# In-place operand sums with a second x staging set, and a half-precision rotary step of the queries, in a two-layer hybrid diffusion kernel

## Chip, cores, metric

The kernel runs on the 8 cores of one Trainium2 chip (dies: cores 0 to 3 and 4 to 7). The metric is device microseconds of the slowest core. Executions of this program fall into two states: fast, and slow, where one die or both run at a lower granted TensorE clock for some per cent longer. A ratio is the mean time of one kernel's fast runs over the mean of the other's fast runs of the same rounds, so it is not quite the ratio of the medians that are quoted beside it.

## The reference, cut to what matters

Two layers over 1280 tokens per core and 2048 channels. Each layer has one input projection that feeds attention, Fourier mixing, a bidirectional scan and a gated MLP; then gates, an output projection, and a squared-ReLU MLP with 8192 hidden channels. Two pieces matter here.

```python
q = _rms(q.reshape(b, L, ATT_HEADS, HEAD_DIM)) * q_g       # 8 query heads of 64
k = _rms(k.reshape(b, L, ATT_KV_HEADS, HEAD_DIM)) * k_g    # 2 key heads of 64
q_use = _rope_2d(q, rows, cols)                            # u1*cos - u2*sin, u1*sin + u2*cos
...
h2 = _rms(x) * (1 + sc2) + sh2
x = x + g2 * (jnp.square(jax.nn.relu(h2 @ w_ff1)) @ w_ff2)
```

## The kernel before

The program is a list of operations with estimated durations. A list scheduler of its own orders them on each engine by those estimates, and the engines then execute that order strictly. One rule of it: outside the block products of the MLP, a matmul group that takes a PSUM tile also waits for whatever the reader of that tile waits for. PSUM is the memory that TensorE writes its results to.

**Query/key projection**, per 128-token tile (10 per layer), three sets of tile buffers, all in 32-bit floats:

```python
S.op("dve", ..., reduce_sum(out=ss, in_=sq))                    # sums of squares of 10 heads
ts_("pool", ss, ss, 1/64, EPS, mult, add)
S.op("pool", 0.6, ... rs = ss ** -0.5)                          # the scheduler is told 0.6 us
tt("dve", qn[:, 0:8], psum_q, rs, mult); tt("dve", qn[:, 8:10], psum_k, rs, mult)
tt("pool", qn[:, 0:8], qn[:, 0:8], gq, mult)                    # norm weight of q
tt("pool", qn[:, 8:10], qn[:, 8:10], gk, mult)
tt("pool", Aa, qn, cos, mult)                                   # 640 wide
for a_ in range(2):
    tt("dve", Bm5[..., a_, :], qn5[..., 1 - a_, :], sin, mult)  # 2 x 320 wide
tt("dve", qr, Aa, Bm, add)                                      # to half precision
# ... five 128x128 transposes on TensorE, copies to qT and kT
```

**MLP.** Both MLP products are computed with 7 instead of 8 half-size block products. A unit is a pair of 128-row output blocks: 112 matmuls of 320 columns. Four sums of operand blocks (T1 to T4) and four of weight blocks are formed on VectorE. There are four quarters of 2048 hidden channels. In each, a first product (to hidden) is followed by a second product (back to x), whose result is added to the 32-bit x that is loaded from memory and stored again.

```python
HTs = [A(40 + 10 * i, [8, 640]) for i in range(4)]    # T1..T4 of the first product's operand (kB, shape)
ATs = [A(80 + 10 * i, [8, 640]) for i in range(4)]    # T1..T4 of the second product's operand
XSt = [hT[:, i, 640:1280].bitcast(F32) for i in range(8)]   # ONE set: 8 tiles of 320 columns of x
def pre_f2(ba, bb):                                   # per unit: 8 loads
    for s_ in range(2):
        for k, (blk, c) in enumerate(...):
            load(XSt[s_ * 4 + k], xs[blk][:, c:c + SUBS], ...)
```

The second product of the last quarter of layer 0 is different: four units only, then ordinary ("dense") blocks, and x is reloaded whole, block by block, into 40 to 120 kB.

## Time and profile before

| | before |
|---|---|
| first six runs | median 5074 us (4990 to 5194), both states |
| fast ones among them | 4990, 4991, 5011 us |
| profiled run (fast) | slowest core 5003.3 us, TensorE busy 4689 us |

The slowest core of this profile is slow for a reason that is not the kernel: cores 0 and 1 were granted a clock of 0.8125 in their last second product, which took 146 and 141 us there against 121.9 us with a full clock.

The top of the page and its first row (busy us, share of the span, instructions), and one row of the chain of work that ended last:

```profile
span 5003.3 us, 84152 instructions; the slowest of 8 cores (4966.0 to 5003.3 us)
...
PE 4689.3 (94%) x29724; PEld 2747.1 (55%) x29724; DVE 2589.0 (52%) x4975; ACT 1465.0 (29%) x2951; POOL 692.5 (14%) x1044
...
PE 77%; DMA 9%; DVE 5%; issue 4%; POOL 2%; ACT 1%; SPq 1%; another core or an unknown queue 0%; DVEq 0%; POOLq 0%; ACTq 0%
```

TensorE (PE) is the bound, and 314 us of idle time are left. Busy time by stretch, for the projection of both layers and for one second product (columns: stretch, its length, busy us of each engine with instructions, granted clock, DMA share, GB/s):

```profile
230.00:310.00 80.00, 59.47 (x343) 31.79 (x340) 48.54 (x89) 20.25 (x47) 61.19 (x59) 0.83 0.42 75
2640.00:2740.00 100.00, 72.09 (x428) 39.43 (x427) 52.01 (x93) 20.82 (x48) 62.94 (x59) 0.92 0.35 80
1704.00:1831.00 127.00, 122.42 (x897) 87.08 (x896) 85.87 (x185) 8.67 (x21) 8.44 (x16) 1.00 0.89 204
```

In the projection TensorE is busy three quarters of the time and the clock sags. One tile in the timeline of layer 1 (start, length, engine, line, operation, count; in brackets the idle time before it and who ended it). L985 is the sum of squares, L746 the small step that adds epsilon, L987 the power, L737 the helper of all elementwise products and sums, L1016 the transposes:

```profile
2663.97 0.89 DVE L737 TENSOR_TENSOR arena<-psum,arena 128x512 f32<-128x512 f32 x2 [1.92 <-POOL arena L987]
...
2664.81 3.45 POOL L737 TENSOR_TENSOR arena<-arena 128x512 f32<-128x512 f32 x3 [0.94 <-DVE arena L737]
...
2666.37 2.23 DVE L737 TENSOR_TENSOR arena<-arena 128x320 f32<-128x320 f32 x2 [1.38 <-POOL arena L737]
...
2668.53 0.81 DVE L985 TENSOR_REDUCE arena<-arena 128x10 f32<-128x640 f32 x1
...
2669.50 0.20 POOL L746 TENSOR_SCALAR arena<-arena 128x10 f32<-128x10 f32 x1 [0.66 <-DVE arena L985]
2669.53 0.84 DVE L737 TENSOR_TENSOR arena<-arena 128x640 f16<-128x640 f32 x1
2669.85 2.36 POOL L987 TENSOR_TENSOR arena<-arena 128x10 f32<-128x10 f32 x1
...
2670.51 0.44 PE L1016 MATMUL psum<-arena 128*128 128x128 f16 x5 [3.00 <-DVE arena L737]
...
2672.32 0.69 DVE L737 TENSOR_TENSOR arena<-psum,arena 128x512 f32<-128x512 f32 x1 [1.95 <-POOL arena L987]
```

Follow the releasers: scaling (VectorE, DVE) releases POOL's three products; they release the sine products; only after these, in VectorE's order, comes the sum of squares of the *next* tile; it releases the power, which releases the next scaling. That is a closed circle of 8.35 us (2663.97 to 2672.32), and TensorE waits at the transposes. The waits say the same for the whole run (waited for, us in total, times, longest):

```profile
PE psum L1016 <- DVE arena L737: 28.7, 15, 3.3
...
PE psum L1601 <- DVE arena L737: 20.6, 18, 2.3
```

L1601 is the 320-column matmul of the MLP. In the chain of 1704 to 1831 us, exactly the second product of the first quarter on this core, x dominates: each load waits for the store of the unit before.

```profile
by line: DMA xs<-arena 50.4%; DMA arena<-xs 21.9%; PE psum L1601 11.3%; SPq L221 10.6%; issue 4.6%; DVE arena L737 2.4%; DVE arena L741 2.3%; ACT arena L751 0.7%; SPq L437 0.3%; SPq L435 0.3%; DVEq L435 0.2%; DVEq L437 0.1%; ACTq L435 0.0%
```

### The profile page before, as it was taken

To read this page: it belongs to the slowest core of one execution; us is meant where nothing else is said; L and a number is where in the kernel's file an instruction comes from. 1 tells how busy PE (TensorE), PEld (TensorE's weight loads), DVE (VectorE), ACT (ScalarE), POOL (GpSimd) and SP (SyncE) were. 2 spreads that over 40 slices of the span, in tenths; PEclk is the share of its full clock that TensorE was granted. 3 is DMA by queue.
4 is the path that set the end of the run, shared out by engine and by line. 5 is a ranking of instruction groups with operands and counts; after the bars stand their busy time and mean duration, and the time that the engine had idled before them with its cause. 6 is when DMAs were issued, how large, how long until landed. Compare 5 with 4: busy or idle time off the path is not lost.

```text
span 5003.3 us, 84152 instructions; the slowest of 8 cores (4966.0 to 5003.3 us)
## 1 busy us (share of the span) xinstructions
PE 4689.3 (94%) x29724; PEld 2747.1 (55%) x29724; DVE 2589.0 (52%) x4975; ACT 1465.0 (29%) x2951; POOL 692.5 (14%) x1044
## 2 busy tenths in 40 slices
PE   1689989999999999999987999899999999999999
PEld 0233435545555767677654344455555567767676
DVE  3345594222236666666665367622223567666656
ACT  2146342111114313132442653311111341414140
POOL 1231142111110000000005013311110000000000
PEclk9789999999999999999998999999999999999998
DMA  7843447775584685858664332666556449484946
GB/s 174 151 92 65 77 96 140 138 137 104 101 172 103 122 191 108 197 107 191 134 167 91 70 65 56 146 125 136 97 94 135 114 86 236 80 223 82 225 84 176
DMA packets 307278, 636.66 MB, mean 127 GB/s; under 512 B 34096, under 2 KB 186160, under 8 KB 306608
## 3 DMA queue, kind: packets, MB, share of 16 engines
q0 software_dynamic: 106560, 368.10, 44.1%
q1 hardware_dynamic: 200304, 263.18, 16.8%
q8 instruction: 244, 4.00, 0.3%
q14 instruction: 170, 1.39, 0.1%
HBM read 875.98 MB, written 123.21 MB: 200 GB/s over the span
## 4 chain that ended last, share of the span: by engine, by line
PE 77%; DMA 9%; DVE 5%; issue 4%; POOL 2%; ACT 1%; SPq 1%; another core or an unknown queue 0%; DVEq 0%; POOLq 0%; ACTq 0%
PE psum L678 42%; PE psum L1601 29%; DMA xs<-arena 4%; DVE arena L737 4%; DMA arena<-wm 2%; DMA arena<-xs 2%; PE psum L1100 1%; PE psum L1039 1%; PE psum L1057 1%; ACT arena L727 1%; DMA arena<-xin 1%; SPq L221 1%; PE psum L810 1%; DVE arena L741 1%; POOL arena L987 1%
## 5 line engine op out<-in xcount | busy, mean ns | idle before, releaser
L678 PE MATMUL psum<-arena 128*128 128x512 f16 (+2 forms) x12992 | 2454.1, 347 | 22.9 <-ACT arena L727 13.3
L678 PEld LDWEIGHTS psum<-arena 128*128 128x128 f16 x12992 | 1253.0, 98 | 1115.5 <-issue 111.0
L1601 PE MATMUL psum<-arena 128*128 128x320 f16 x13216 | 1830.6, 302 | 27.0 <-DVE arena L737 20.6
L1601 PEld LDWEIGHTS psum<-arena 128*128 128x128 f16 x13216 | 1300.7, 99 | 556.4 <-issue 40.3
L737 DVE TENSOR_TENSOR arena<-arena 128x1024 f16<-128x1024 f16 (+9 forms) x1648 | 923.5, 579 | 234.7 <-ACT arena L727 141.8
L727 ACT ACTIVATE arena<-arena 128x320 f32<-128x320 f32 (+8 forms) x1374 | 681.2, 519 | 891.9 <-DVE arena L737 461.2
L737 DVE TENSOR_TENSOR arena<-psum,arena 128x320 f32<-128x320 f32 (+4 forms) x1346 | 656.9, 491 | 479.9 <-PE psum L1601 358.1
L741 DVE SCALAR_TENSOR_TENSOR arena<-arena,psum 128x512 f16<-128x512 f16 (+3 forms) x492 | 297.9, 607 | 1043.3 <-ACT arena L727 1042.9
L727 ACT ACTIVATE arena<-psum 128x512 f16<-128x512 f32 (+6 forms) x738 | 382.9, 520 | 1389.5 <-PE psum L678 1304.5
L751 ACT COPY arena<-psum 128x320 f32<-128x320 f32 (+6 forms) x384 | 169.9, 448 | 1034.7 <-DVE arena L741 482.1
L741 DVE SCALAR_TENSOR_TENSOR arena<-arena 128x320 f32<-128x320 f32 (+10 forms) x665 | 354.7, 554 | 170.9 <-DMA arena<-xs 82.8
L221 POOL DMA_DIRECT2D arena<-w x256 | 136.7, 534 | 1860.6 <-PE psum L1601 1668.3
L221 POOL DMA_DIRECT2D arena<-wm x192 | 105.9, 552 | 1010.3 <-PE psum L810 813.7
L727 ACT ACTIVATE arena<-psum,arena 128x512 bf16<-128x512 f32 x320 | 203.0, 684 | 122.9 <-PE psum L1039 122.6
L741 DVE SCALAR_TENSOR_TENSOR arena<-psum,arena 128x320 f32<-128x320 f32 (+2 forms) x240 | 143.2, 605 | 178.5 <-PE psum L678 120.5
L737 POOL TENSOR_TENSOR arena<-arena 128x512 bf16<-128x512 bf16 (+2 forms) x160 | 187.3, 1187 | 107.6 <-ACT arena L751 55.0
L737 DVE TENSOR_TENSOR arena<-arena,psum 128x512 f16<-128x512 f32 (+3 forms) x232 | 135.2, 608 | 20.7 <-ACT arena L727 13.1
L810 PE MATMUL psum<-arena 128*32 128x512 f16 x768 | 79.3, 420 | 57.5 <-DMA arena<-wm 44.4
L752 DVE CAST arena<-psum 128x512 f16<-128x512 f32 (+4 forms) x102 | 53.5, 527 | 106.5 <-PE psum L1100 51.8
L883 PE MATMUL psum<-arena 128*128 128x1 f32 x80 | 11.9, 267 | 94.1 <-DVE arena L737 92.5
L746 DVE TENSOR_SCALAR arena<-arena 128x128 f32<-128x128 f32 (+10 forms) x124 | 54.9, 466 | 67.8 <-ACT arena L751 39.7
L221 POOL DMA_DIRECT2D arena<-wg x128 | 72.3, 565 | 123.5 <-PE psum L678 67.3
(89 smaller groups left out, 1049.7 us busy)
## 6 DMA issues: line engine op xcount, KB each, us to landing
arena<-w POOLq DMA_DIRECT2D x256, 512.0 KB, 7.0
arena<-wm POOLq DMA_DIRECT2D x192, 512.0 KB, 7.1
arena<-xs SPq DMA_DIRECT2D x448, 160.0 KB, 5.1
arena<-wg POOLq DMA_DIRECT2D x128, 512.0 KB, 8.2
xs<-arena SPq DMA_DIRECT2D x384, 160.0 KB, 6.5
xs<-arena SPq DMA_DIRECT2D x96, 256.0 KB, 4.3
arena<-xin SPq DMA_DIRECT2D x32, 640.0 KB, 19.2
arena<-xs SPq DMA_DIRECT2D x32, 640.0 KB, 8.6
```

The lines of the kernel that those rows point to most:

```text
L221: return self.op(q, issue, (lambda e, o=out, a=in_, k=kw: e.dma_start(out=lz(o), in_=lz(a), **k)), r, w, prio, dma=nbytes, q=q, tag=tag)
L678: ins = e.matmul(o, lhsT=lhs(kc), rhs=rhs(kc), start=kc == 0, stop=kc == nk - 1)
L727: return e.activation(out=lz(o), in_=lz(i), func=func, scale=scale, **kw)
L737: lambda e: e.tensor_tensor(out=lz(o), in0=lz(a), in1=lz(b), op=op), r=r, w=w, prio=S.p - boost, tag=tag)
L741: lambda e: e.scalar_tensor_tensor(out=lz(o), in0=lz(a), scalar=sc, in1=lz(b), op0=op0, op1=op1),
L746: lambda e: e.tensor_scalar(out=lz(o), in0=lz(a), scalar1=s1, scalar2=s2, op0=op0, op1=op1),
L751: return S.op("act", tact(n), lambda e: e.copy(out=lz(o), in_=lz(i)), r=r, w=w, prio=S.p - boost, tag=tag)
L752: return S.op(eng, tpool(n) if eng == "pool" else tdve(n, ps, x), lambda e: e.tensor_copy(out=lz(o), in_=lz(i)), r=r, w=w, prio=S.p - boos ...
L810: ins = e.matmul(ps.ap()[32 * j:32 * j + 32, :], lhsT=scT[:, kc, :], rhs=w[:, 512 * j:512 * j + 512], start=kc == 0, stop=kc == 15)
L987: S.op("pool", 0.6, lambda e, rs=rs, ss=ss: e.tensor_tensor(out=rs, in0=ss, in1=mhalf[:, 0:10], op=ALU.pow), r=[ss, mhalf], w=[rs], prio=S ...
L1039: ins = e.matmul(sc.ap()[:, hf * 512:hf * 512 + n], lhsT=kT[64 * hf:64 * hf + 64, kb * 128:(kb + 1) * 128], rhs=qT[64 * hf:64 * hf + 64, j ...
L1601: ins = e.matmul(ps.ap()[:, 0:SUBS], lhsT=wv(kc), rhs=rhs(kc), start=first and kc == 0, stop=kc == 7, skip_group_check=True)
```

## The change

Intent: take the query norm weight and half of the rotary arithmetic off POOL and into half precision on VectorE (tables that already carry the weight), with four tile buffers. In the MLP, write T1 over the operand block that it no longer needs, and spend the freed space on a second set of x tiles.

```diff
+            tt("dve", COSQ, COS, bc_in(gq, 10), ALU.mult, ...)        # tables with the norm weight, f16
+            ... SINQ likewise, with the weight of the other half
-            bases = (140.5, 40, 52)
+            bases = (141, 40, 48.5, 57)
-                S.op("pool", 0.6, ... ALU.pow ...)
+                S.op("pool", 2.2, ... ALU.pow ...)
-                tt("pool", qn[:, 0:8], qn[:, 0:8], bc_in(gq, 8), ALU.mult, 512, ...)
-                tt("pool", Aa, qn, bc_in(ct, 10), ALU.mult, 640, ...)
-                (2x) tt("dve", Bm5..., qn5..., sin, ALU.mult, 320, ...)
-                tt("dve", qr, Aa, Bm, ALU.add, 640, ...)
+                tt("dve", Aq, qn, COSQ, ALU.mult, 512, ...)           # queries: f16, VectorE
+                (2x) tt("dve", Bq..., qn..., SINQ, ALU.mult, 256, ...)
+                tt("dve", qr[0:512], Aq, Bq, ALU.add, 512, ...)
+                tt("pool", Ak, kn, cos, ALU.mult, 128, ...)           # keys: f32, POOL
+                (2x) tt("pool", Bk..., kn..., sin, ALU.mult, 64, ...)
+                tt("pool", qr[:, 4, :], Ak, Bk, ALU.add, 128, ...)
 ... cut ...
-        HTs = [A(40 + 10 * i, [8, 640]) for i in range(4)]
-        ATs = [A(80 + 10 * i, [8, 640]) for i in range(4)]
+        HTs = [hT[:, 0:8, 640:1280]] + [A(40 + 10 * i, [8, 640]) for i in range(3)]
+        ATs = [mT[:, 0:8, 640:1280]] + [A(80 + 10 * i, [8, 640]) for i in range(3)]
+        # T1 of the first product is formed after the dense blocks have read hT
-            XSt = [hT[:, i, 640:1280].bitcast(F32) for i in range(8)]
+            XSt = [[A(base + 2.5 * k, [640], F32) for k in range(4)] for base in (70, 110)]
+            # pre_f2: 4 loads of 640 columns into the set not in use; one store of 640 per block half
+                at = ATs if q < 3 or last else [A(110, [8, 640])] + ATs[1:]
```

In the short second product of layer 0 the operand must stay intact, so T1 gets a place of its own: 110 kB.

More of the change, by code (lines that the diff above doesn't have):

```diff
@@ L961, in attn_proj @@
             load(V[:, 0:2, :].rearrange("p a b -> p (a b)"), ctxv[l], 128 * 1024, q="pool", w=[V[:, 0:2, :]])
-            bases = (140.5, 40, 52)
+            COSQ = A(157.5, [10, 64])
+            SINQ = A(158.75, [10, 64])
+            gq = gqk[:, 0:64]
+            gk = gqk[:, 64:128]
+            tt("dve", COSQ, COS, bc_in(gq, 10), ALU.mult, 640, [COS, gq], [COSQ])
+            s5 = lambda v: v.rearrange("p t (r a d) -> p t r a d", r=2, a=2)
+            g4 = gq.rearrange("p (r a d) -> p r a d", r=2, a=2)
+            for a_ in range(2):
+                tt("dve", s5(SINQ)[:, :, :, a_, :], s5(SIN)[:, :, :, a_, :], g4[:, :, 1 - a_, :].unsqueeze(1).to_broadcast([128, 10, 2, 16]), ALU.mult, 320,
+                   [SIN, gq], [SINQ])
+            bases = (141, 40, 48.5, 57)
             for t in range(NT):
-                base = bases[t % 3]
-                if base == 140.5:
-                    base = 141.0
+                base = bases[t % 4]
                 sq = A(base, [10, 64], F32)
-                qn = A(base + 2.5, [10, 64], F32)
-                Aa = A(base + 5, [10, 64], F32)
-                Bm = A(base + 7.5, [10, 64], F32)
-                qr = A(base + 10, [5, 128])
-                vt = A(base + 10, [128], F32) if False else A(base + 11.25 - 0.25, [128], F32) if False else sq.rearrange("p a b -> p (a b)")[:, 0:128]
-                ss, rs, tw = stt[2 * (t % 3) % 6][:, 0:10], stt[(2 * (t % 3) + 1) % 6][:, 0:10], None
+                qn = A(base + 2.5, [8, 64])
+                kn = A(base + 3.5, [2, 64], F32)
+                Aq = A(base + 4, [8, 64])
+                Bq = A(base + 5, [8, 64])
+                Ak = A(base + 6, [2, 64], F32)
+                Bk = A(base + 6.5, [2, 64], F32)
+                qr = A(base + 7, [5, 128])
+                vt = sq.rearrange("p a b -> p (a b)")[:, 0:128]
+                ss, rs = stt[2 * (t % 3)][:, 0:10], stt[2 * (t % 3) + 1][:, 0:10]
                 cols = slice(t * 128, (t + 1) * 128)
@@ L986, in attn_proj @@
                 ts_("pool", ss, ss, 1.0 / 64, EPS, ALU.mult, ALU.add, 10, [ss], [ss], boost=BOOST)
-                S.op("pool", 0.6, lambda e, rs=rs, ss=ss: e.tensor_tensor(out=rs, in0=ss, in1=mhalf[:, 0:10], op=ALU.pow), r=[ss, mhalf], w=[rs], prio=S.p - BOOST)
+                S.op("pool", 2.2, lambda e, rs=rs, ss=ss: e.tensor_tensor(out=rs, in0=ss, in1=mhalf[:, 0:10], op=ALU.pow), r=[ss, mhalf], w=[rs], prio=S.p - BOOST)
                 dv = dtv[:, t, :]
@@ L992, in attn_proj @@
                 h8 = lambda a: a.rearrange("p (h d) -> p h d", d=64)
-                tt("dve", qn[:, 0:8], lambda bq=bq: h8(bq.ap()[:, 0:512]), bc_mid(rs[:, 0:8], 64), ALU.mult, 512, [bq, rs], [qn[:, 0:8]], ps=True, boost=BOOST)
-                tt("dve", qn[:, 8:10], lambda bk=bk: h8(bk.ap()[:, 0:128]), bc_mid(rs[:, 8:10], 64), ALU.mult, 128, [bk, rs], [qn[:, 8:10]], ps=True, boost=BOOST)
+                tt("dve", qn, lambda bq=bq: h8(bq.ap()[:, 0:512]), bc_mid(rs[:, 0:8], 64), ALU.mult, 512, [bq, rs], [qn], ps=True, boost=BOOST)
@@ L995, in attn_proj @@
+                tt("dve", kn, lambda bk=bk: h8(bk.ap()[:, 0:128]), bc_mid(rs[:, 8:10], 64), ALU.mult, 128, [bk, rs], [kn], ps=True, boost=BOOST)
                 cp("act", vt, lambda bk=bk: bk.ap()[:, 128:256], 128, [bk], [vt], boost=BOOST)
                 S.dma("sp", nv_o[l, cols, :], vt, 65536, r=[vt])
-                gq = gqk[:, 0:64]
-                gk = gqk[:, 64:128]
-                tt("pool", qn[:, 0:8], qn[:, 0:8], bc_in(gq, 8), ALU.mult, 512, [qn[:, 0:8], gq], [qn[:, 0:8]])
-                tt("pool", qn[:, 8:10], qn[:, 8:10], bc_in(gk, 2), ALU.mult, 128, [qn[:, 8:10], gk], [qn[:, 8:10]])
@@ L1001, in attn_proj @@
-                S.dma("sp", nk_o[l, cols, :], qn[:, 8:10].rearrange("p a b -> p (a b)"), 65536, r=[qn[:, 8:10]])
-                ct = COS[:, t, :]
-                tt("pool", Aa, qn, bc_in(ct, 10), ALU.mult, 640, [qn, ct], [Aa])
-                qn5 = qn.rearrange("p h (r a d) -> p h r a d", r=2, a=2)
-                Bm5 = Bm.rearrange("p h (r a d) -> p h r a d", r=2, a=2)
-                st4 = SIN[:, t, :].rearrange("p (r a d) -> p r a d", r=2, a=2)
-                for a_ in range(2):
-                    tt("dve", Bm5[:, :, :, a_, :], qn5[:, :, :, 1 - a_, :], st4[:, :, a_, :].unsqueeze(1).to_broadcast([128, 10, 2, 16]), ALU.mult, 320,
-                       [qn, SIN[:, t, :]], [Bm])
@@ L1010, in attn_proj @@
-                tt("dve", qr.rearrange("p a b -> p (a b)"), Aa.rearrange("p a b -> p (a b)"), Bm.rearrange("p a b -> p (a b)"), ALU.add, 640, [Aa, Bm], [qr])
+                tt("pool", kn, kn, bc_in(gk, 2), ALU.mult, 128, [kn, gk], [kn])
+                S.dma("sp", nk_o[l, cols, :], kn.rearrange("p a b -> p (a b)"), 65536, r=[kn])
+                x5 = lambda v: v.rearrange("p h (r a d) -> p h r a d", r=2, a=2)
+                x4 = lambda v: v.rearrange("p (r a d) -> p r a d", r=2, a=2)
+                tt("dve", Aq, qn, bc_in(COSQ[:, t, :], 8), ALU.mult, 512, [qn, COSQ[:, t, :]], [Aq], x=2)
@@ new lines, in attn_proj @@
+                for a_ in range(2):
+                    tt("dve", x5(Bq)[:, :, :, a_, :], x5(qn)[:, :, :, 1 - a_, :], x4(SINQ[:, t, :])[:, :, a_, :].unsqueeze(1).to_broadcast([128, 8, 2, 16]), ALU.mult, 256,
+                       [qn, SINQ[:, t, :]], [Bq])
+                f2 = lambda v: v.rearrange("p a b -> p (a b)")
+                tt("dve", f2(qr)[:, 0:512], f2(Aq), f2(Bq), ALU.add, 512, [Aq, Bq], [qr[:, 0:4]], x=2)
+                tt("pool", Ak, kn, bc_in(COS[:, t, :], 2), ALU.mult, 128, [kn, COS[:, t, :]], [Ak])
@@ L1011, in attn_proj @@
+                for a_ in range(2):
+                    tt("pool", x5(Bk)[:, :, :, a_, :], x5(kn)[:, :, :, 1 - a_, :], x4(SIN[:, t, :])[:, :, a_, :].unsqueeze(1).to_broadcast([128, 2, 2, 16]), ALU.mult, 64,
+                       [kn, SIN[:, t, :]], [Bk])
+                tt("pool", qr[:, 4, :], f2(Ak), f2(Bk), ALU.add, 128, [Ak, Bk], [qr[:, 4, :]])
                 bt = PS("q")
@@ L1526, in spill, with tsums @@
             S.dma("sp", d[fc][:, t0:t0 + n], src, 128 * n * 4, r=[src], w=xkeys(fc, t0, n) if dst is None else [], tag="xst")
-        HTs = [A(40 + 10 * i, [8, 640]) for i in range(4)]
-        ATs = [A(80 + 10 * i, [8, 640]) for i in range(4)]
+        HTs = [hT[:, 0:8, 640:1280]] + [A(40 + 10 * i, [8, 640]) for i in range(3)]
+        ATs = [mT[:, 0:8, 640:1280]] + [A(80 + 10 * i, [8, 640]) for i in range(3)]
         SL = [A(184 + 2 * i, [1024]) for i in range(4)]
-        def tsums(act, Ts, i):
+        def tsums(act, Ts, i, part=3):
             b11, b12 = act[:, i, 0:640], act[:, i, 640:1280]
@@ L1535, in tsums @@
             t1, t2, t3, t4 = (t[:, i, :] for t in Ts)
-            for o, x, y in ((t1, b12, b11), (t3, b22, b12), (t2, b22, t1), (t4, b21, t2)):
-                tt("dve", o, x, y, ALU.subtract, 640, [x, y], [o], x=2)
+            ops = ((t3, b22, b12, ALU.subtract), (t2, t3, b11, ALU.add), (t4, b21, t2, ALU.subtract), (t1, b12, b11, ALU.subtract))
+            for o, x, y, op in (ops[:3] if part & 1 else ()) + (ops[3:] if part & 2 else ()):
+                tt("dve", o, x, y, op, 640, [x, y], [o], x=2)
         sslot = [[0, 1, 2, 3]]
+        xpar = [0]
         def ssums(ra, rb, p):
@@ L1661, in after_o @@
                     for i in range(8):
-                        tsums(hT, HTs, i)
+                        tsums(hT, HTs, i, 1)
             ev = ev_res(l, 32, after_o)
@@ L1684, in epi_f1 @@
                 if done1.get(i, 0) == 4 and done1.get(i + 8, 0) == 4:
-                    tsums(mT, ATs, i)
-            XSt = [hT[:, i, 640:1280].bitcast(F32) for i in range(8)]
+                    tsums(mT, at, i)
+            XSt = [[A(base + 2.5 * k, [640], F32) for k in range(4)] for base in (70, 110)]
             def res(x, b, ps, g0, g1, c):
@@ L1698, in pre_f2 @@
             def pre_f2(ba, bb):
-                for s_ in range(2):
-                    for k, (blk, c) in enumerate(((ba, s_ * SUBS), (ba, 640 + s_ * SUBS), (bb, s_ * SUBS), (bb, 640 + s_ * SUBS))):
-                        load(XSt[s_ * 4 + k], xs[blk][:, c:c + SUBS], 128 * SUBS * 4, r=xkeys(blk, c, SUBS), prio=S.p + 50, tag="xld")
+                xpar[0] ^= 1
+                for k, (blk, c) in ((3, (bb, 640)), (0, (ba, 0)), (1, (ba, 640)), (2, (bb, 0))):
+                    load(XSt[xpar[0]][k], xs[blk][:, c:c + 640], 128 * 640 * 4, r=xkeys(blk, c, 640), prio=S.p + 60 - 12, tag="xld")
             def epi_f2(dst):
                 def f(blk, c, b, ps, s_, k):
-                    x = XSt[s_ * 4 + k]
-                    res(x, b, ps, *gcol(blk), c)
-                    spill(blk, c, SUBS, x, dst)
+                    x = XSt[xpar[0]][k]
+                    res(x[:, s_ * SUBS:s_ * SUBS + SUBS], b, ps, *gcol(blk), c)
+                    if s_ == 1:
+                        spill(blk, c - SUBS, 640, x, dst)
                 return f
@@ L1733, in layer @@
                     dense(b1[5:], hT, ev_f1, tag="ff1")
+                    for i in range(8):
+                        tsums(hT, HTs, i, 2)
                     for i in range(3):
-                        tsums(mT, ATs, i)
+                        tsums(mT, at, i)
                     sunits([pair1(i) for i in range(3, 8)], hT, HTs, epi_f1, tag="sf1")
@@ L1739, in layer @@
                 if q < 3 or last:
-                    sunits([pair2(i) for i in range(8)], mT, ATs, epi_f2(None if q < 3 else y_o), pre=pre_f2, tag="sf2")
+                    sunits([pair2(i) for i in range(8)], mT, at, epi_f2(None if q < 3 else y_o), pre=pre_f2, tag="sf2")
                 else:
                     reload_x(range(8), xs, True)
-                    sunits([(i, i + 4, w2[l, q, i], w2[l, q, i + 4]) for i in range(4)], mT, ATs, epi_x, tag="sf2")
+                    sunits([(i, i + 4, w2[l, q, i], w2[l, q, i + 4]) for i in range(4)], mT, at, epi_x, tag="sf2")
                     reload_x(range(8, 16), xs, True)
```

## The prediction

> **What bounds the kernel now.** TensorE: busy 4689 of 5003 us (busy table), 77% of the chain of waits. Only its idle time can be won. About 150 of the 314 us idle is start-up, left alone. Two touched stages:
>
> 1. Query/key projection. In 230–310 us TensorE is busy 59.5 of 80 us at clock 0.83; in 2640–2740 us, 72 of 100 at 0.92 (busy time by stretch). In the timeline a 128-token tile takes 8.3 us, though its matmuls need about 6 (16x0.216 + 16x0.127 + 0.44). Each period is a closed circle between VectorE and POOL: pow (2.3), scaling from PSUM (0.9), POOL norm weight (1.5), POOL cosine product (1.85) beside VectorE sine products (2x1.1), the next tile's reduce (0.81). The transposes wait 28.7 us for VectorE (waits). The 320-element sine product takes 1065 ns, the 640-element add 829. The Trainium skill ("GPSIMD Engine Reference", Specifications) says GpSimd shares SBUF interfaces with VectorE instructions of two SBUF inputs; the sine product runs beside POOL's product, so the trace agrees.
>
> 2. Second MLP product. x has one set of staging tiles, so loads wait for the spills of the unit before: the chain in 1715–1850 us is 47% stores of x, 21% loads. Yet TensorE loses only 7.4, 6 and 5 us in three stretches of layer 0 and 8.6 in all of the last MLP; other cores often 2 to 3 per stretch.
>
> **Removed, added, moved.** Per tile POOL loses the query weight (1.1) and the 640-wide cosine product, keeps pow plus short key operations (0.4 each): 6–6.5 us becomes about 4.5. VectorE gets half-precision query products, about 0.4 + 2x0.5 + 0.4 (estimated from the f32 durations), for 2.23 + 0.83. Tables cost about 2 us per layer. The scheduler is told pow's true length, so transposes move later in TensorE's order, and a fourth buffer lets them. I expect 6–6.6 us per tile. In the MLP the additions are as many and as large; the freed space allows two x sets and half as many, twice as large transfers. A quarter of the operand sums now waits until the dense blocks have read the operand: about 3 us of VectorE at that junction, needed by the fourth product only, so nearly hidden.
>
> **On the critical path.** Projection: 15–22 us per layer, 35 in both, plus about 6 because the clock no longer drops in gaps (the skill's "TensorE: Matmul & The Clock Gate", Part 1: an idle array is throttled; the trace has 0.5 to 0.83 in slices with gaps). MLP: 7 to 20 by core, 14 taken. Lost: 3 to 5 (junction, other order). Sum about 50 us, 1.0%. More than 85 is not there to be won in these stages.
>
> **Prediction.** Fast runs before are 4990 to 5011 us; after, near 4940. The quoted median mixes in slow runs (5137 to 5194), so I allow for some: 4950 us, range 4890 to 5045. Faster by over 2%: 0.10; within 2%: 0.88; slower by over 2%: 0.02.
>
> **Right if** the tile period falls to about 6.5 us, the transposes' waits for VectorE below 10, TensorE busy over 90% in the projection at a clock near 1; the chain leaves the x stores and loads and TensorE idles under 2 us per second product. **Wrong if** the period stays near 8 us (POOL and VectorE blocking each other, or pow still in a circle), doubled transfers collide with weight loads, the late sums stall the junction, or the reordered attention and scan stages lose or gain tens of us.

## The result and the profile after

| | before | after |
|---|---|---|
| all runs of these rounds | median 5077 us (20 runs) | median 4928 us (4903 to 5154, 10 runs) |
| fast runs, ratio | 1 | 0.9835, interval 0.9810 to 0.9859 |
| profiled run (fast), slowest core | 5003.3 us | 4902.8 us |
| profiled run, median of the cores' spans | 4977.5 us | 4895.7 us |

The seven fast runs among the ten have a mean of 4916 us, so the gain is 1.65%, some 82 us.

```profile
span 4902.8 us, 83279 instructions; the slowest of 8 cores (4881.9 to 4902.8 us)
...
PE 4646.0 (95%) x29724; PEld 2732.6 (56%) x29724; DVE 2574.1 (53%) x5001; ACT 1467.6 (30%) x2951; POOL 667.0 (14%) x1084
...
PE 86%; DMA 4%; DVE 4%; issue 3%; POOL 2%; ACT 1%; another core or an unknown queue 0%; SPq 0%; DVEq 0%; POOLq 0%; ACTq 0%
```

The same number of matmuls, and TensorE's share of the chain is up by nine points (77% to 86%). The stretches that answer to those before (a second product, then the projection of both layers):

```profile
1684.00:1806.00 122.00, 122.00 (x900) 87.88 (x899) 90.64 (x194) 8.82 (x22) 8.44 (x16) 1.00 0.86 214
220.00:295.00 75.00, 67.07 (x440) 37.25 (x437) 43.04 (x111) 25.25 (x55) 49.81 (x82) 0.98 0.51 88
2604.00:2680.00 76.00, 67.12 (x425) 36.90 (x423) 43.43 (x109) 26.00 (x56) 47.57 (x79) 0.96 0.41 84
```

The second product is now solid: 122.00 busy of 122.00. One tile of the projection (L998 is the power, L996 the sum of squares, L1028 the transposes, the others as before):

```profile
2618.00 0.89 DVE L737 TENSOR_TENSOR arena<-psum,arena 128x512 f16<-128x512 f32 x2 [0.58 <-POOL arena L998]
2618.81 2.03 DVE L737 TENSOR_TENSOR arena<-arena 128x512 f16<-128x512 f16 x4
...
2619.03 1.05 POOL L737 TENSOR_TENSOR arena<-arena 128x128 f32<-128x128 f32 x2 [1.14 <-DVE arena L737]
...
2620.76 0.81 DVE L996 TENSOR_REDUCE arena<-arena 128x10 f32<-128x640 f32 x1
2620.80 1.39 POOL L737 TENSOR_TENSOR arena<-arena 128x64 f32<-128x64 f32 x3
...
2622.45 0.44 PE L1028 MATMUL psum<-arena 128*128 128x128 f16 x5 [0.29 <-POOL arena L737]
2622.63 1.98 POOL L998 TENSOR_TENSOR arena<-arena 128x10 f32<-128x10 f32 x1
...
2624.71 0.89 DVE L737 TENSOR_TENSOR arena<-psum,arena 128x512 f16<-128x512 f32 x2 [0.82 <-POOL arena L998]
```

From scaling to scaling it is 6.7 us here (6.0 to 6.7 in the tiles around it). The waits of the transposes and of the MLP's matmuls, and the chain in the second product, which no longer touches x:

```profile
PE psum L1028 <- POOL arena L737: 6.2, 11, 0.9
...
PE psum L1615 <- DVE arena L737: 3.4, 2, 2.2
...
PE psum L1028 <- DVE arena L737: 0.3, 1, 0.3
```

```profile
by line: PE psum L1615 100.1%
```

Where the time went, stage by stage, worked out from the traces of all eight cores (medians). "Projection" runs from the start of the first 272-column matmul of the layer to the end of its last transpose. "Behind it" runs to the last matmul of the scan. "Boundary" runs from the last 320-column matmul of layer 0 to the first 272-column matmul of layer 1. The last two columns are the first two experiments.

| stage, us | before | after | proj_only | mlp_only |
|---|---|---|---|---|
| projection, layer 0 | 90.9 | 69.6 | 69.7 | 91.4 |
| projection, layer 1 | 95.6 | 74.4 | 73.4 | 92.7 |
| attention to scan behind it, layers 0 / 1 | 479.5 / 476.3 | 479.0 / 472.9 | 482.1 / 473.2 | 479.7 / 481.6 |
| gates to dense blocks of the first product, both | 1647.3 | 1643.0 | 1652.1 | 1645.2 |
| six whole first products, summed | 735.1 | 730.2 | 735.4 | 731.4 |
| seven whole second products, summed | 873.7 | 852.1 | 890.1 | 852.1 |
| boundary of the layers | 132.4 | 123.1 | 130.5 | 122.6 |

The differences of before and after add to 86 us against 82 in the medians of the spans; medians of parts do not add exactly. Of these, 42.5 are the projection, 26.5 the MLP products, 9.3 the boundary, and 8 the small rows.

### The profile page after: what moved, and what is told of

Its sections match the earlier page's. It is cut to its first block, busy times and chain, and to the rows that moved or that the text cites. A ratio compares the mean times of both kernels' runs of the same rounds, so it can differ in the third digit from the quotient of the medians.

```text
span 4902.8 us, 83279 instructions; the slowest of 8 cores (4881.9 to 4902.8 us)
## 1 busy us (share of the span) xinstructions
PE 4646.0 (95%) x29724; PEld 2732.6 (56%) x29724; DVE 2574.1 (53%) x5001; ACT 1467.6 (30%) x2951; POOL 667.0 (14%) x1084
## 4 chain that ended last, share of the span: by engine, by line
PE 86%; DMA 4%; DVE 4%; issue 3%; POOL 2%; ACT 1%; another core or an unknown queue 0%; SPq 0%; DVEq 0%; POOLq 0%; ACTq 0%
PE psum L678 43%; PE psum L1615 36%; DVE arena L737 3%; DMA arena<-wm 2%; PE psum L1112 1%; PE psum L1051 1%; PE psum L1069 1%; PE psum L810 1%; DMA arena<-xin 1%; ACT arena L727 1%; PE psum L1071 1%; POOL arena L998 1%; DVE arena L741 1%; POOL arena L737 1%; DMA arena<-wf 0%
## 5 line engine op out<-in xcount | busy, mean ns | idle before, releaser
L678 PE MATMUL psum<-arena 128*128 128x512 f16 (+2 forms) x12992 | 2448.8, 346 | 19.9 <-ACT arena L727 8.6
L678 PEld LDWEIGHTS psum<-arena 128*128 128x128 f16 x12992 | 1249.8, 98 | 1107.9 <-issue 107.8
L1615 PE MATMUL psum<-arena 128*128 128x320 f16 x13216 | 1798.3, 299 | 5.0 <-DVE arena L737 3.4
L737 DVE TENSOR_TENSOR arena<-arena 128x1024 f16<-128x1024 f16 (+9 forms) x1674 | 905.8, 558 | 213.5 <-ACT arena L727 113.7
L737 DVE TENSOR_TENSOR arena<-psum,arena 128x320 f32<-128x320 f32 (+5 forms) x1346 | 658.4, 491 | 533.8 <-PE psum L1615 449.0
L741 DVE SCALAR_TENSOR_TENSOR arena<-arena,psum 128x512 f16<-128x512 f16 (+4 forms) x492 | 297.9, 606 | 1049.3 <-ACT arena L727 1049.2
L727 ACT ACTIVATE arena<-psum 128x512 f16<-128x512 f32 (+7 forms) x738 | 383.5, 520 | 1395.6 <-PE psum L678 1295.8
L737 POOL TENSOR_TENSOR arena<-arena 128x512 bf16<-128x512 bf16 (+4 forms) x200 | 162.6, 827 | 122.1 <-ACT arena L751 58.4
L883 PE MATMUL psum<-arena 128*128 128x1 f32 x80 | 11.9, 267 | 94.3 <-DVE arena L737 92.7
L810 PEld LDWEIGHTS psum<-arena 128*32 128x32 f16 x768 | 20.8, 96 | 122.2 <-issue 120.5
```

What stands on the lines that cost most here:

```text
L678: ins = e.matmul(o, lhsT=lhs(kc), rhs=rhs(kc), start=kc == 0, stop=kc == nk - 1)
L727: return e.activation(out=lz(o), in_=lz(i), func=func, scale=scale, **kw)
L737: lambda e: e.tensor_tensor(out=lz(o), in0=lz(a), in1=lz(b), op=op), r=r, w=w, prio=S.p - boost, tag=tag)
L741: lambda e: e.scalar_tensor_tensor(out=lz(o), in0=lz(a), scalar=sc, in1=lz(b), op0=op0, op1=op1),
L810: ins = e.matmul(ps.ap()[32 * j:32 * j + 32, :], lhsT=scT[:, kc, :], rhs=w[:, 512 * j:512 * j + 512], start=kc == 0, stop=kc == 15)
L1615: ins = e.matmul(ps.ap()[:, 0:SUBS], lhsT=wv(kc), rhs=rhs(kc), start=first and kc == 0, stop=kc == 7, skip_group_check=True)
```

## The experiments

All kernels were correct. A stage without idle time repeats to 0.1 us where the clock is full: in the changed kernel the first six second products take 121.7 us on nearly every core. The sum of the projection and the stage behind it, used below, repeats to 4 us between profiles of kernels with the same projection.

### proj_only and mlp_only: the two halves alone

```diff
 proj_only: kernel before + the new projection, nothing of the MLP part
 mlp_only:  changed kernel with the old projection
```

> The new query/key projection in the kernel before, nothing else. Stage times are medians over the eight cores. Theory (the parts act each in its own stage and add up): the projection stage falls from 90.9 and 95.6 us (layers 0 and 1) to 69 to 71 and 73 to 76; the second MLP products stay near 124 us each and the layer boundary near 132 us; the fast runs gain 42 to 52 us, ratio 0.990 to 0.992. Rival (most of the gain beyond my forecast comes from the new order of attention and scan behind the projection): ratio below 0.988, with those two stages shorter by over 8 us.

> The change without its projection part. Theory: projection as before (91 and 96 us), second MLP products 121.7 us each on the median core instead of about 124, boundary between the layers 123 instead of 132 us; fast runs gain 25 to 38 us, ratio 0.992 to 0.995. Rival (MLP gain is what I forecast, 14 us, and the boundary belongs to the projection part): ratio above 0.996, boundary near 132.

Measured: proj_only 0.9942 (interval 0.9894 to 0.9989, from two fast runs of 4988 and 4969 us), mlp_only 0.9917 (0.9888 to 0.9946), just outside the 0.992 to 0.995 expected. The stages are in the table above. The halves act each in its own stage. The projection falls to 69.7 and 73.4 us without the MLP part; the second products, the boundary and most of the first products improve without the projection part. The time of proj_only is a miss beside its expectation, though inside the interval. The profile shows why: its second products took 16 us more than in the profile of before (890 against 874), which hides a part of the 43 us that its projection shows. Near 124 us each was expected, and 127 came. That this is chance of the x transfers, and not a result of the edit, is likely but not shown. Across five profiles with one x set of 320-column tiles, the seven second products sum to 873.7, 874.7, 878.8, 883.2 and 890.1 us; with two sets every profile has 852.1 to 852.5.

### old_place and new_place: the line that is easy to overlook

```diff
 old_place (in the changed kernel):
-  at = ATs if q < 3 or last else [A(110, [8, 640])] + ATs[1:]
+  at = ATs if q < 3 or last else [A(80 + 10 * i, [8, 640]) for i in range(4)]
 new_place (in the kernel before):
-  ATs = [A(80 + 10 * i, [8, 640]) for i in range(4)]
+  ATs = [A((110, 80, 90, 100)[i], [8, 640]) for i in range(4)]
```

> The changed kernel with the four operand sums of the last, short second product of layer 0 laid in the order of the kernel before (first sum at the place of x rows 8 and 9). Theory (the boundary gain comes from the place of the sums: which x rows can be reloaded first): TensorE again waits 5 to 7 us for a load of x right after the last 320-column matmul of layer 0, boundary 129 to 132 us instead of 123; all else as in the changed kernel. Rival (the boundary gain comes from the lighter queue of x transfers): no such wait, boundary stays near 123.

> The kernel before with only the place of the four operand sums of the second products changed (first sum in the last place, the others moved up). Theory: the 5 to 7 us wait for x after the last 320-column matmul of layer 0 is gone and the boundary takes 123 to 126 us instead of 132; nothing else moves by over 3 us. Rival: the wait stays, boundary near 132.

Measured (one look each): boundary 132.6 us in old_place and 122.4 us in new_place. TensorE's timeline on core 2 at the boundary, for before, after, old_place and new_place in this order (L678 are the dense blocks):

```profile
2510.41 8.85 PE L1601 MATMUL psum<-arena 128*128 128x320 f16 x64 [1.11 <-DVE arena L737]
2519.10 7.07 PE L678 MATMUL psum<-arena 128*128 128x512 f16 x32
2533.40 41.16 PE L678 MATMUL psum<-arena 128*128 128x512 f16 x216 [7.24 <-DMA arena<-xs]
```

```profile
2474.37 8.85 PE L1615 MATMUL psum<-arena 128*128 128x320 f16 x64 [1.11 <-DVE arena L737]
2483.06 46.01 PE L678 MATMUL psum<-arena 128*128 128x512 f16 x248
```

```profile
2478.51 8.85 PE L1615 MATMUL psum<-arena 128*128 128x320 f16 x64 [1.11 <-DVE arena L737]
2487.20 7.07 PE L678 MATMUL psum<-arena 128*128 128x512 f16 x32
2500.25 41.86 PE L678 MATMUL psum<-arena 128*128 128x512 f16 x216 [5.98 <-DMA arena<-xs]
```

```profile
2522.78 8.85 PE L1601 MATMUL psum<-arena 128*128 128x320 f16 x64 [1.11 <-DVE arena L737]
2531.47 13.78 PE L678 MATMUL psum<-arena 128*128 128x512 f16 x71
```

The wait follows the place, and each of the two runs changed nothing else: on the eight cores it is 4.1 to 9.5 us in before and 4.2 to 6.9 us in old_place, and no core has it in after and new_place. In the old order x blocks 8 and 9, which the dense blocks need first, lie under T1, the third sum to be freed. In the new one they lie under T2, the first to be freed. In new_place the second products moved by 9.5 us to 883 us, more than the 3 us expected; they lie within the spread of one-set kernels given above, and the one look took 5008 us in all, so the gain at the boundary did not show in its total.

### pow_only and pow06: what the scheduler is told

```diff
 pow_only (kernel before):    - S.op("pool", 0.6, ... pow ...)   + S.op("pool", 2.2, ... pow ...)
 pow06 (changed kernel):      - S.op("pool", 2.2, ... pow ...)   + S.op("pool", 0.6, ... pow ...)
```

> The kernel before with one number changed: the scheduler is told 2.2 us for the power on POOL in the projection instead of 0.6; the instructions are the same, in another order. Theory (POOL and VectorE really have too much serial work per tile): projection 84 to 95 us per layer instead of 91 and 96, tile period still over 7.5 us. Rival (the closed circle came from a wrong order alone): projection falls to 70 to 78 us.

> The changed kernel with the scheduler told 0.6 us again for that power. Theory (less work on POOL is what counts, order second): projection 70 to 78 us per layer instead of 69.6 and 74.4. Rival (the order is what counts): 85 us or more.

### three_buf and f32_q: the fourth buffer and half precision

```diff
 three_buf:  - bases = (141, 40, 48.5, 57)     + bases = (141, 40, 48.5)
 f32_q:      three buffers (141, 40, 52); qn, Aq, Bq of the queries in F32, same instructions
```

> The changed kernel with three tile buffers instead of four. Theory (the fourth buffer only lets transposes lag): projection 70 to 76 us per layer, at most 3 us above the changed kernel. Rival (buffers bound it): over 80 us.

> The changed kernel with three buffers and the query step in full precision (the folded tables stay in half precision). Theory (half precision saves VectorE about 1 us a tile, but VectorE is busy only 57% of the stage): at most 5 us per layer above the three-buffer run. Rival (half precision is a main part of the gain): 85 us or more per layer, tile period over 7.5 us.

Measured in these four (one look each) and in the neighbours, medians of the cores. Transposes can slip behind the projection's end, so the sum with the stage behind is given too:

| kernel | projection 0 / 1, us | with the stage behind 0 / 1, us |
|---|---|---|
| before | 90.9 / 95.6 | 570.5 / 571.9 |
| pow_only | 76.0 / 84.2 | 554.2 / 552.8 |
| pow06 | 80.8 / 77.1 | 558.2 / 554.3 |
| f32_q | 74.1 / 75.4 | 550.8 / 554.7 |
| three_buf | 69.4 / 72.8 | 552.2 / 546.8 |
| after | 69.6 / 74.4 | 548.6 / 547.3 |

One number in the scheduler, with not an instruction changed, saves 14.9 and 11.4 us in the projection and 16.3 and 19.1 us with the stage behind: 35 of the 46 us that the whole new projection brings by that measure. The same edit in two_lines (below) gave the same sums within 0.5 us. For layer 0 the rival of pow_only was right; layer 1 lies at the edge of the theory's range. The waits of the transposes in pow_only, against 28.7 us before:

```profile
PE psum L1016 <- DVE arena L737: 5.9, 9, 0.9
```

POOL's timeline of pow_only shows what the order does. Counted from 0, the power at 2654.26 is tile 3's; it comes before the cosine product of tile 2, which is the first of the four operations at 2656.22. So the circle is open here.

```profile
2648.39 1.98 POOL L987 TENSOR_TENSOR arena<-arena 128x10 f32<-128x10 f32 x1
2650.35 2.58 POOL L737 TENSOR_TENSOR arena<-arena 128x640 f32<-128x640 f32 x2
...
2653.60 0.20 POOL L746 TENSOR_SCALAR arena<-arena 128x10 f32<-128x10 f32 x1
2653.88 0.41 POOL L737 TENSOR_TENSOR arena<-arena 128x128 f32<-128x128 f32 x1
2654.26 1.99 POOL L987 TENSOR_TENSOR arena<-arena 128x10 f32<-128x10 f32 x1
2656.22 5.21 POOL L737 TENSOR_TENSOR arena<-arena 128x640 f32<-128x640 f32 x4
```

It is not open in every tile. Of the nine steps from tile to tile, the next power comes before this tile's cosine product in one step per layer in before, but in seven (layer 0) and four (layer 1) in pow_only. From power to power the open steps take 5.7 and 6.3 us, the others 8.4 and 7.7 us (medians over the cores; 8.3 us in before). That is why layer 1 gains less.

The converse, pow06, keeps the lighter work and the wrong estimate. It loses 11.2 and 2.7 us against the changed kernel, more in layer 0 than the theory allowed. In its trace POOL still takes the operations nearly tile by tile, as in the changed kernel: with either estimate the circle there stays closed, but is shorter, 6.9 us from power to power in pow06 and 6.1 to 6.2 in the changed kernel (which part of the new order makes this last difference was not separated). So lighter work shortens the circle and the right order opens it in a part of the tiles, and their savings overlap: order alone is worth 35 us, work and buffers alone (pow06) 30, both together 46. The fourth buffer is worth nothing that can be seen (three_buf is not slower in the projection). Half precision is worth 4.7 and 2.6 us in the projection (f32_q against three_buf); with the stage behind, the sign differs between the layers.

### one_set and two_set_320: second set or larger transfers

```diff
 one_set:      - XSt = [... for base in (70, 110)]   + XSt = [... for base in (70, 70)]
 two_set_320:  two sets; every load and store split into two of 320 columns
```

> The changed kernel with both sets of x tiles at the same place: one set, transfers still 640 wide. Theory (the second set frees TensorE: loads no longer wait for the spill of the unit just before): second products lose again, 124 to 132 us instead of 121.7 on the median core, and the chain of waits passes through x stores and loads. Rival (fewer and larger transfers are what helps): below 122.5 us.

> The changed kernel with two sets of x tiles but transfers of 320 columns, as many as before. Theory: second products stay at 121.7 to 122.5 us on the median core. Rival (fewer and larger transfers are what helps): 124 us or more.

Measured (one look each): the seven second products sum to 879.9 us with one set of large transfers (125.7 on average) and to 852.5 us with two sets of small ones. The chains in the second product of the first quarter, on core 4, of one_set (1671 to 1801 us) and of two_set_320 (1690 to 1811 us):

```profile
by line: PE psum L1615 77.0%; DMA xs<-arena 8.9%; issue 4.7%; DMA arena<-xs 3.9%; DVE arena L737 3.9%; DVE arena L741 1.7%; DVEq L435 0.2%; DVEq L437 0.0%; SPq L435 0.0%; SPq L437 0.0%
```

```profile
by line: PE psum L1615 100.1%
```

And the busy time in these stretches, in the same order (second number: TensorE busy):

```profile
1671.00:1801.00 130.00, 123.69 (x899) 86.65 (x897) 86.05 (x186) 8.70 (x21) 8.44 (x16) 1.00 0.83 201
```

```profile
1690.00:1811.00 121.00, 121.00 (x893) 87.18 (x891) 90.81 (x193) 8.17 (x20) 8.48 (x16) 1.00 0.87 205
```

The second set is what counts; half as many, twice as large transfers add nothing here. One_set keeps the other edits of this part too (the loads in another order and with another priority, the sums by another formula), so these are not what pays either. The run of two_set_320 as a whole took 4980 us. The chip granted less clock in its first products (0.93 to 1.00 by core and product, with almost no idle time of TensorE there) and in some second products of cores 0 and 1 (0.96 to 0.98), so only the medians of its second products are used.

### two_lines: the two findings put into the kernel before

```diff
-  S.op("pool", 0.6, ... pow ...)
+  S.op("pool", 2.2, ... pow ...)
-  ATs = [A(80 + 10 * i, [8, 640]) for i in range(4)]
+  ATs = [A((110, 80, 90, 100)[i], [8, 640]) for i in range(4)]
```

> The kernel before with two numbers changed: the scheduler is told 2.2 us for the power in the projection, and the operand sums of the second products are laid in the other order of places. No instruction is added or removed. The projection and the attention, Fourier, gMLP and scan work behind it are summed here, since transposes can slip past the end of the projection: before 570 and 572 us in layers 0 and 1, changed kernel 549 and 547, the single edit of the power 554 and 553. Theory (order alone breaks the circle): 552 to 557 us in both layers, boundary 122 to 125 us, second products still about 125 us each; the fast runs gain 35 to 50 us, ratio 0.990 to 0.993. Rival (the single look of the power edit was chance): sums of 562 us or more, ratio above 0.996.

Measured: 0.9918 (0.9859 to 0.9977), sums 554.6 and 552.8 us, boundary 123.0 us, second products 125.5 us on average. Two numbers, without one instruction added or removed, bring about half of the gain of the whole change (0.8% of 1.65%; from two fast runs, so the interval is wide).

### v2: the last key addition to VectorE

```diff
-  tt("pool", qr[:, 4, :], f2(Ak), f2(Bk), ALU.add, 128, ...)
+  tt("dve",  qr[:, 4, :], f2(Ak), f2(Bk), ALU.add, 128, ...)
```

> The changed kernel with the last addition of the key's rotary step on VectorE instead of POOL. The transposes of the changed kernel wait 6.2 us in all for POOL's key step. Theory (POOL's key step is the last releaser, VectorE has room): projection 66 to 70 and 71 to 75 us, transposes wait under 3 us for POOL; 2 to 6 us in all, too little for the timed rounds to tell from the changed kernel: ratio to before 0.981 to 0.986. Rival (the scheduler sets the transposes earlier and the waits come back from VectorE): projection 72 us or more in layer 0.

Measured: projection 67.2 and 72.2 us against 69.6 and 74.4 in the changed kernel; all other stages within 3 us of it. Ratio to before 0.9807 (0.9770 to 0.9845), at the edge of the expected range and "unclear" as a verdict, since the interval spans 2%. The transposes no longer wait for POOL; all that is left in the waits is:

```profile
PE psum L1028 <- DVE arena L737: 2.5, 7, 0.5
```

By the stages it is 4.6 us better in the projection than the changed kernel, but only 1.4 us with the stage behind. The timed intervals of the two overlap and come from different rounds, so that it is faster as a whole is not shown.

## Why the prediction was right or wrong

Forecast: fast runs near 4940 us, a gain of about 50 us or 1.0%, within 2%. Measured: 4916 us, 82 us or 1.65%, within 2%; the median of all runs, 4928 us, lies in the stated range. Both stages gained by the waits that were named; the size was short by 32 us. Point by point:

- **Projection, 35 us plus 6 us of clock: right in size.** Measured 42.5 us, the share of the clock not apart. That the size fits is partly luck: by the sums with the stage behind, lighter work alone (pow06) gave 30 us and the order alone 35. The tile period fell to 6.0 to 6.7 us (forecast 6.0 to 6.6), and the transposes' waits for VectorE to 0.3 us (forecast below 10); instead they wait 6.2 us for POOL's key step. TensorE is busy 88 to 89% in the stage, just short of the "over 90%" forecast; the clock is 0.95 to 0.96 over the whole stage (medians of the cores, 0.85 and 0.88 before). The sagging clock before fits the Trainium skill ("TensorE: Matmul & The Clock Gate", Part 1: an array that idles is throttled); in the stretches shown it was 0.83 and 0.92 with gaps, and 0.98 and 0.96 with fewer.
- **Its cause: half right.** I named the closed circle, but booked the gain mainly to the 1.5 to 2 us of POOL work taken away per tile. pow_only shows that the estimate for the power, 0.6 us told against 2.0 to 2.3 us measured, had closed the circle; with the stage behind, correcting it alone brings 35 of 46 us. "A fourth buffer lets them": three_buf shows that it is not needed.
- **MLP, 14 us taken: mis-sized.** The term measured 26.5 us on the median core: 21.6 in the second products, 4.9 in the first products behind them (735.1 to 730.2 us). The waits were the right ones, and the 14 us match TensorE's idle time in the seven second products of before (14.6 us on the median core). But the length lost there was larger than the idle time, since the busy time around the gaps grew too, in part with the clock (0.97 to 0.99 in some of them); and 4.2 us more were idle in the first products. The forecast counted idle time alone. And x waits differ from profile to profile: against the five one-set profiles above the second products gained 22 to 38 us. "TensorE idles under 2 us per second product" held but for one product on one core (2.9 us): elsewhere it is zero or at most 1.1 us.
- **"Lost: 3 to 5 (junction, other order)": this step failed.** Nothing was lost. The late T1 costs 0.1 us at the junction (the five first units take 76.2 us against 76.1). In place of a loss the boundary of the layers gained 9.3 us, from the place of the sums of one product, which I had read in the diff and not followed to the reload of x. Another 8 us came in small steps elsewhere, whose cause no experiment separated.
- **"More than 85 is not there to be won in these stages"** held: the two stages gave 69 us.
- **Sine product beside POOL's product: right.** In the projections of before, on all cores, a 320-element sine product takes 478 ns with POOL idle (median of 32). Beside the 640-wide cosine product it depends on which began first: the 112 that began just before it took 493 ns, and the 138 that began while it ran took 1637 ns, each ending 0.34 to 0.35 us after it. This agrees with the Trainium skill, "SBUF — State Buffer", sections "Who interferes with whom" and "Summary: rules for kernel authors": the pair of ports is an exclusive lock, and the second to issue blocks until the first has finished. Beside the power it takes 493 ns (14 of them). So the order of pow_only helps VectorE too: there 152 of the 320 sine products run beside the power, and their mean falls from 988 to 790 ns.

## What to carry to other kernels

Where a scheduler orders the engines from estimates, measure each estimate against the trace before changing the arithmetic: one operation told at under a third of its length closed a circle that looked like too much work. When buffers are reloaded under a deadline, lay first what is needed first under what is freed first; the order of four places was worth 9 us. Double staging pays by letting a load skip one store; larger transfers alone did not pay here.

## What the Trainium skill lacked or had wrong

- "GPSIMD Engine Reference" has a measured cost for an element-wise add, but none for the power: here one power of 128x10 f32 on POOL takes 1.96 to 2.63 us (median 2.33 before, 1.98 after), and one of 128x4 1.03 us.
- That page and "SBUF — State Buffer" state that POOL and VectorE contend; the price here was 1637 against 478 ns for a 320-element f32 product. "SBUF — State Buffer" (Terms) says that the pair is held for the full instruction; here the power, which reads SBUF and lasts 2 us or more, did not hold it so long: in pow_only 136 sine products ran wholly inside a power and took 475 to 499 ns.
- "VectorE: DVE Perf Modes" gives rates by mode and, for f32 `tensor_tensor`, a formula that it checks at 512 and 2048 elements; it has no figure for the short strided pieces of a rotary step. Here 256 elements in runs of 16 take 423 ns in f32 with POOL idle (the formula gives 424) and 284 ns in f16, and 512 contiguous f16 elements 416 ns.
- "TensorE: Matmul & The Clock Gate" (the note on the peak-current limiter in Part 1) says that dense matmuls on three cores of a die bring the whole die to 13/16 of the clock and hold it there while the load lasts. Here eleven of the fourteen profiles, all eight cores busy, never show this clock, the changed kernel's among them (0.986 to 0.989 over the run). Three show it in parts: in the profile of before, cores 0 and 1 ran their last 115 and 146 us at 0.8125 while cores 2 and 3 of the same die stayed at 1.0. The page's figure fits the slow run of 5818 us: one die had a mean of 0.81.
